# A two-layer hybrid decoder step on one core: dummy matmuls and squares at the beginning, and four edits of the recurrent mixer's order

## The chip, the cores and the metric

The kernel runs on one core of a Trainium2 chip. The time is the device time of one execution in microseconds (us); several runs are shown with their median, lowest and highest. The profile is of one execution.

## The reference

One inference step of a trunk of two layers, for a prompt of 256 tokens and 8 samples of 8 tokens (320 token columns in all), model width 1024. Every layer is a half-weighted SwiGLU network (width 2816), a mixer, and a second SwiGLU network, each with a norm before and after it:

```python
h = swiglu(rmsnorm(x, ffn1_norm_pre[l]), ffn1_w_up[l], ffn1_w_down[l])
x = x + 0.5 * rmsnorm(h, ffn1_norm_post[l])
h, cb, rh, S = mixer(rmsnorm(x, mix_norm_pre[l]), conv_st[l], rg_st[l], dn_st[l], ...)
x = x + rmsnorm(h, mix_norm_post[l])
h = swiglu(rmsnorm(x, ffn2_norm_pre[l]), ffn2_w_up[l], ffn2_w_down[l])
x = x + 0.5 * rmsnorm(h, ffn2_norm_post[l])
```

The mixer projects its input once (`h @ w_in`), runs a causal convolution of width 4 over the first columns (recurrence input, q, k, v), and joins two groups of heads:

- a gated linear recurrence of width 512 (a scan over time), times a gelu gate;
- four heads of a gated delta rule of width 128: queries, keys and values with silu, q and k of unit length; in chunks of 64 tokens a triangular system is solved, then states are carried on, `S = S * exp(gl) + (k * decay)^T @ v_new`; the output `o` is normed, `rmsnorm(o, dn_norm_w) * silu(z)`.

Both groups are concatenated and go through `w_out`. Outputs are the tokens after a final norm and all states of both layers, for the prompt and for the samples.

## The kernel before

**Numbers in two parts.** Activations lie with features on the 128 partitions, `x[128, 8, 320]`. A weight block of 1024 x 128 is loaded into a buffer `raw` by SyncE's (SP's) queue and split: ScalarE (ACT) writes the high part `wh` (L130), VectorE (DVE) the low part `wl = raw - wh` (L135). The activations are split in the same way, `xh` and `xl`. TensorE (PE) adds three products for each of 8 slices: `xh wh`, `xh wl`, `xl wh`. So one block is a *unit* of 24 matmuls of 128 x 128 by 320 columns (L158).

**Order.** PE's order is written out by hand. `Fill` (L161) holds a phase's list of units; `F(n)` issues the next n matmuls of that list and loads two units ahead (`prefetch`), `F.to(i)` all up to unit i. For the other engines a planner orders the instructions by its own forecast of when each can start: of those that are ready it takes the one that comes first in the program, and `high_priority(offset=n)` puts an instruction n places earlier. The order is then fixed, and each engine works through its own strictly. There are five `raw` buffers, three of each of `wh` and `wl`; PSUM's eight banks are three `mm`, four `sm` and one `st`.

**Beginning** (L1302 to L1423). Tokens come in rows, are transposed on PE (`xin`, L1332) and copied to `x`. The first three units are loaded in halves, and their matmuls are issued by hand, four at a time (`mm4`); ACT's and DVE's orders are written out here too. 13 dummy matmuls (`dummies`, L1327) on a constant run ahead. After them the squares of the tokens give the row factor `rs`, which PE turns (L1421) and ACT stores as `rsb2`; up to there the units' results are unscaled. `F(46)` stands between.

**Mixer** (L616 on). The list has 33 units: unit 0 is 8 columns (weights `wsr`, split into `wsh` and `wsl` in L625 and L626), then four each of k, q, v, recurrence input, z and gate, then eight of `w_out`. Each result of k, q, v and recurrence goes through `conv` (L662): two multiplications by `rsb2` on DVE (L674, L675), one step on ACT (L684), three on DVE (L686) and the copy or silu on ACT (L707, L708). Between the fill matmuls, PE runs the delta rule: products of k with k, a solve in doubling steps (`quads`, L910) whose links on ACT and DVE carry offset `HPO = 400` (called the chain below), and products of k with q (`qk`, L932, PE line L936), which need the convolved queries of all four heads. `scale_o` (L1047) computes the factor of the normed output: squares on ACT, `fs` on DVE, the power -1/2 on GpSimd (POOL), the scaling on ACT (L1057). `rg_scan` (L1073) runs the recurrence, with four roots on ACT.

The samples' state comes last: for each of two pairs of heads (p) four matmuls of 32 rows by 512 columns into four `sm` banks (L1212), added to the state by DVE (L1216), then written out by POOL's queue. `finish_o` (L1222) transposes the scaled output on PE (L1225), multiplies by silu(z) (L1227) and splits it; `split_r` (L1232) splits the recurrence output after its gate product (L735 to L737). `FL` holds the numbers of fill matmuls between these steps: `FL[19]` and `FL[20]` before each p, `FL[21]` and `FL[22]` around `finish_o`.

```python
F(FL[19 + p])
ps2 = [smtile() for _ in range(4)]
for j in range(4):
    r = slice(32 * j, 32 * j + 32)
    pe.matmul(ps2[j], kd[r, u], ve[r], start=True, stop=True)
```

Of the kernel before, what the change touches and what calls it, by code (L numbers as in the profile page):

```python
# [28 lines left out]
CVW = PADW - 3  # L29
NU = 10  # L30
HPO = 400
HPK = 300
HPW = 0
HPB = 60
# [22 lines left out]
PS = [(0, 1, 2), (0, 2, 1), (0, 2, 1)]  # L57
PO = [0, 0, -1, 0, 1, 1, -1, 2, 2, -1, 2, 1, -1]
XC = []
FL = [14, 37, 32, 9, 15, 8, 0, 14, 0, 11, 10, 8, 6, 4, 4, 6, 21, 1, 8, 0, 16, 6, 11]  # L60
FZ = [11, 11, 11, 22, 8, 17]
FY = [10, 10, 5, 3, 11, 6]

# [18 lines left out]
def trunk(ctx, tc, x_prompt, x_sample, state_conv, state_rglru, state_delta,  # L82
# [34 lines left out]
    def sttile():  # L117
        return stp.tile([128, 512], F32, name="st")

    def wload(src, r0, nk, c0, spare=False, sub=None, tok=None):  # L120
        raw = wts.tile([128, 8, 128], F32, name="raw", bufs=5)
        nc.sync.dma_start(raw[:, :nk], src[r0:r0 + nk * 128, c0:c0 + 128].rearrange("(k p) c -> p k c", p=128))
        if spare:
            w = aux.tile([128, 16, 128], F32R, name="aux")
            wh, wl = w[:, 0:8], w[:, 8:16]
        else:
            wh = wts.tile([128, 8, 128], F32R, name="wh")
            wl = wts.tile([128, 8, 128], F32R, name="wl")
        with tc.high_priority(offset=HPW):
            act(wh[:, :nk], raw[:, :nk], *((AF.Copy,) if tok is None or tok[0] else (AF.Identity, tok[1]())))  # L130
            if tok is not None and tok[0]:
                with tc.high_priority(offset=HPX):
                    stt(wl, raw, tok[1](), wh.bitcast(F32), op0=OP.add, op1=OP.subtract)
                return wh, wl
            (sub or dve).tensor_sub(wl[:, :nk], raw[:, :nk], wh[:, :nk].bitcast(F32))  # L135
        return wh, wl

    class Blk:
# [477 lines left out]
    class Mixer:  # L616
        def __init__(self, l, side):
# [4 lines left out]
            wsh = tmp.tile([128, 8, 8], F32R, name="wsh", bufs=1)  # L622
            wsl = tmp.tile([128, 8, 8], F32R, name="wsl", bufs=1)
            nc.sync.dma_start(wsr, w_in[l][:, 3072:3080].rearrange("(k p) c -> p k c", p=128))
            act(wsh, wsr, AF.Copy)  # L625
            dve.tensor_sub(wsl, wsr, wsh.bitcast(F32))  # L626
            units = [Unit(lambda a: (wsh, wsl), Blk(smtile, 8), xsplit, done=lambda ps: self.scal_done(ps))]
            for base, fn in ((1024, self.k_done), (512, self.q_done), (1536, self.v_done), (0, self.rg_done),
                             (2560, self.z_done), (2048, self.gate_done)):
                for h in range(4):  # L630
                    units.append(Unit(lambda a, c=base + 128 * h: wload(w_in[l], 0, 8, c, a, tok=(False, xtoken) if c == 512 else None), Blk(smtile if base + h == 1027 else mmtile), xsplit,
                                      done=lambda ps, h=h, fn=fn: fn(h, ps)))
            for m in range(KD):
                units.append(Unit(lambda a, m=m: wload(w_out[l], 0, 8, m * 128), Blk(mmtile if m < 3 else ptile),
# [109 lines left out]
        def run(self):  # L744
# [302 lines left out]
            def scale_o(u0, n):  # L1047
                for i in range(n):
                    act(sqtile()[:, 0:128], por[:, u0 + i], AF.Square, accum_out=oss[:, u0 + i:u0 + i + 1])
                us = slice(u0, u0 + n)  # L1050
                stt(fs[:, us], oss[:, us], 1.0 / 128, qss[:, us], op0=OP.mult, op1=OP.add)
                pool.tensor_tensor(fs[:, us], fs[:, us], mhalf[:, us], op=OP.pow)
                for i in range(n):
                    if SO:
                        dve.tensor_scalar(por[:, u0 + i], por[:, u0 + i], fs[:, u0 + i:u0 + i + 1], None, op0=OP.mult)
                    else:
                        act(por[:, u0 + i], por[:, u0 + i], AF.Copy, scale=fs[:, u0 + i:u0 + i + 1])  # L1057
# [15 lines left out]
            def rg_scan():  # L1073
# [10 lines left out]
                    stt(rt[:, c], a2, 1.0, rt[:, c], op0=OP.add, op1=OP.mult)  # L1084
                for c in range(4):
                    act(rt[:, c], rt[:, c], AF.Sqrt, scale=0.25)
                    dve.tensor_mul(it[:, c], it[:, c], rt[:, c])
                    h0 = vec[:, 2, 32 * l + c:32 * l + 32:4]
                    ts_ = mt([128, NB], "ts_", 2)
                    dve.tensor_mul(ts_, aa[:, c, NP:T:SL], h0)  # L1090
                    dve.tensor_add(it[:, c, NP:T:SL], it[:, c, NP:T:SL], ts_)
                    pool.memset(aa[:, c, 0:1], 0.0)
                    pool.memset(aa[:, c, NP:T:SL], 0.0)
                    dve.tensor_tensor_scan(xr[:, c], aa[:, c], it[:, c], 0.0, op0=OP.mult, op1=OP.add)  # L1094
# [109 lines left out]
            for p in range(2):  # L1204
                u = 8 + p
                S = SS[p]
                ve = ves[p]
                F(FL[19 + p])
                ps2 = [smtile() for _ in range(4)]
                for j in range(4):  # L1210
                    r = slice(32 * j, 32 * j + 32)
                    pe.matmul(ps2[j], kd[r, u], ve[r], start=True, stop=True)  # L1212
                for j in range(4):
                    sv4 = S[:, j // 2, 4 * (j % 2):4 * (j % 2) + 4].rearrange("p b e -> p (b e)")
                    with tc.high_priority(offset=HPO):
                        dve.tensor_add(sv4, sv4, ps2[j])  # L1216
                for h in range(2):
                    nc.gpsimd.dma_start(dn_s[l][:, 2 * p + h].rearrange("b d e -> d b e"), S[:, h])
            mh[1] = mt([128, 4, T], "kd", 1, F32R)
            ml[1] = mt([128, 4, T], "vn", 1, F32R)  # L1220
# [83 lines left out]
    raws = [wts.tile([128, 8, 128], F32, name="raw", bufs=5) for _ in range(n)]  # L1304

    def xload(c):
        nc.sync.dma_start(xtok[:, 0, c], x_prompt[0, 0:128, c])
        nc.sync.dma_start(xtok[:, 1, c], x_prompt[0, 128:256, c])
        nc.scalar.dma_start(xtok[0:64, 2, c], x_sample.rearrange("b s d -> (b s) d")[:, c])

    def whalf(i, hf):
        c0 = (i % 2) * DFF + (i // 2) * 128
# [11 lines left out]
    dve.tensor_copy(ph.gh[:, 0], bc(ones[:, 0:1], T))  # L1324
    gp0 = ph.fp.tile([128, 16], F32, name="gp0", bufs=1)

    def dummies(m):  # L1327
        ps = sttile()
        for _ in range(m):
            pe.matmul(ps[:, :T], ph.gh[:, 0, :128], ph.gh[:, 0], start=True, stop=True)  # L1330

    def xin(k):  # L1332
        ps = smtile()
# [9 lines left out]
    with tc.manual_schedule(engines={mybir.EngineType.Activation, mybir.EngineType.DVE}):  # L1343
# [27 lines left out]
        act(gp0, ps[:, 0:16], AF.Copy)  # L1371
        dummies(4)
        pt = [xin(j) for j in range(4)]
        for hf in range(2):
            k0 = 4 * hf
            xcopy(k0, pt[0])
            xcopy(k0 + 1, pt[1])
            xcopy(k0 + 2, pt[2])
            xh_(k0)
            wh_(0, hf)  # L1380
            xh_(k0 + 1)
            xcopy(k0 + 3, pt[3])
            xh_(k0 + 2)
            xh_(k0 + 3)
            wl_(0, hf)
            for i in range(1, n):
                wh_(i, hf)
            mm4(0)
            xl_(k0)
            xl_(k0 + 1)  # L1390
            mm4(0)
            if hf == 0:
                pt = [xin(4), xin(5)]
            mm4(1)
            xl_(k0 + 2)
            xl_(k0 + 3)
            mm4(2)
            wl_(1, hf)
            mm4(0)
            if hf == 0:  # L1400
                pt += [xin(6), xin(7)]
            mm4(1)
            wl_(2, hf)
            mm4(1)
            mm4(2)
            mm4(2)
        F.prefetch(5)
        ss = tmp.tile([128, 3], F32, name="rs")
        dve.memset(ss, 1.0)
        hpf = hp.rearrange("p k t -> p (k t)")  # L1410
        for t, r in enumerate((128, 128, 64)):
            act(hpf[0:r, :D], xtok[0:r, t], AF.Square, accum_out=ss[0:r, t:t + 1])
    F.i = n
    late_done, F.u[n].done = F.u[n].done, None
# [71 lines left out]
```

## Time and profile before

| | us |
|---|---|
| median of 3 runs (lowest to highest) | 1279.9 (1279.4 to 1281.31) |
| profiled execution, its own time | 1281.22 |
| its span, first to last instruction | 1279.3 |
| PE busy in the span, matmuls | 1250.1 (98%), 9812 instructions |
| DVE busy | 853.2 (67%) |
| ACT busy | 698.1 (55%) |
| POOL busy | 109.3 (9%) |
| `wl`, L135, DVE | 321 times, mean 1198 ns |
| `wh`, L130, ACT | 316 times, mean 1036 ns |
| mean granted clock of PE | 0.987 |

The page has the busy time of each engine, the span in 40 slices, DMA queues, the chain of work that ended last, and the costliest groups of instructions. Further views answer for a stretch or an engine: the timeline (start, duration, line, tile written and read, shape, count; in brackets the idle time before it and what ended it), the waits (total, times, longest), and the busy times of all engines in chosen stretches with the granted clock. Matmuls are pipelined, so their durations overlap: the distance from start to start is their cost. The low level of PE's clock is 1.2 GHz, the full one 2.4.

### The profile page before, as it was taken

Reading aid. Unit: us, or ns where it says so; the run is one execution under the profiler, and the core shown is the slowest. Engines: PE = TensorE matmul, PEld = TensorE weight load, DVE = VectorE, ACT = ScalarE, POOL = GpSimd, SP = SyncE. Lnnn points to the kernel's source line nnn. Section 1 sums busy time; section 2 is a strip of 40 time slices with the busy share of each in tenths; the row PEclk is TensorE's granted clock in tenths of the full one; section 3 lists DMA queues with packets and bytes.
Section 4 is the critical chain, followed back from the end, with each engine's and each line's share of the span. In section 5 each row is a group of like instructions: output and inputs, shape, how many; then the busy total and the mean of one; then the engine's idle time right before and its main releaser. Section 6 shows DMA issues by size and latency. Waiting matters only on the chain.

```text
span 1279.3 us, 24478 instructions
## 1 busy us (share of the span) xinstructions
PE 1250.1 (98%) x9812; PEld 1216.5 (95%) x9812; DVE 853.2 (67%) x1541; ACT 698.1 (55%) x1220; POOL 109.3 (9%) x241
## 2 busy tenths in 40 slices
PE   9999999998999999999999999999899999999996
PEld 7999999998979999999999999999899899999995
DVE  4976644799776866654486665459986877666444
ACT  5654444675686644444464444446749675444443
POOL 1100000232130100000000000013411210000000
PEclk9999999998989999999999999999999899999998
DMA  8555555563346455555645555575332655555551
GB/s 207 156 171 161 161 152 167 137 159 84 84 131 174 118 165 160 161 152 168 181 118 159 162 165 153 164 193 141 89 84 59 186 152 166 164 165 156 147 143 42
DMA packets 356470, 187.26 MB, mean 146 GB/s; under 512 B 9034, under 2 KB 353436, under 8 KB 356356
## 3 DMA queue, kind: packets, MB, share of 16 engines
q1 hardware_dynamic: 353124, 178.12, 49.3%
q0 software_dynamic: 2672, 6.65, 1.9%
q8 instruction: 77, 1.26, 0.4%
q10 hardware_dynamic: 560, 0.93, 0.2%
q14 instruction: 37, 0.30, 0.1%
HBM read 179.16 MB, written 6.51 MB: 145 GB/s over the span
## 4 chain that ended last, share of the span: by engine, by line
PE 90%; DVE 6%; ACT 2%; DMA 1%; issue 1%; POOL 0%; SPq 0%; DVEq 0%; ACTq 0%
PE mm L158 44%; PE sm L158 38%; PE sm L914 2%; PE st L231 1%; DMA raw<-in_ffn_w_up_dram 1%; PE sm L978 1%; DVE co L686 1%; DVE wl L135 1%; DVE xr L1094 1%; DVE aux L1216 0%; PE sm L936 0%; DVE nA L921 0%; DVE DN L828 0%; PE sm L1070 0%; DVE bt L425 0%
## 5 line engine op out<-in xcount | busy, mean ns | idle before, releaser
L135 DVE TENSOR_TENSOR wl<-raw,wh 128x1024 fp32r<-128x1024 f32 x321 | 384.4, 1198 | 214.1 <-ACT wh L130 209.8
L130 ACT ACTIVATE wh<-raw 128x1024 fp32r<-128x1024 f32 (+1 forms) x316 | 326.6, 1036 | 367.5 <-issue 127.0
L158 PE MATMUL mm<-xh,wl 128*128 128x320 f32 x976 | 294.8, 306 | 7.8 <-DVE wl L135 7.8
L158 PE MATMUL mm<-xh,wh 128*128 128x320 f32 x976 | 295.6, 308 | 1.0 <-ACT wh L1352 0.8
L158 PE MATMUL mm<-xl,wh 128*128 128x320 f32 x976 | 287.8, 305 | 0.0
L158 PE MATMUL sm<-xh,wh 128*128 128x320 f32 x720 | 215.6, 299 | 0.0
L158 PE MATMUL sm<-xl,wh 128*128 128x320 f32 x720 | 215.5, 299 | 0.0
L158 PE MATMUL sm<-xh,wl 128*128 128x320 f32 x720 | 215.4, 299 | 0.0
L158 PEld LDWEIGHTS mm<-xh,wl 128*128 128x128 f32 x976 | 186.2, 192 | 12.9 <-DVE wl L135 8.7
L158 PEld LDWEIGHTS mm<-xh,wh 128*128 128x128 f32 x976 | 186.7, 192 | 6.0 <-issue 1.5
L158 PEld LDWEIGHTS mm<-xl,wh 128*128 128x128 f32 x976 | 183.8, 192 | 2.7 <-issue 1.1
L158 PEld LDWEIGHTS sm<-xh,wl 128*128 128x128 f32 x720 | 136.1, 189 | 0.3 <-DVE wl L135 0.3
L158 PEld LDWEIGHTS sm<-xh,wh 128*128 128x128 f32 x720 | 136.1, 189 | 0.0
L158 PEld LDWEIGHTS sm<-xl,wh 128*128 128x128 f32 x720 | 136.1, 189 | 0.0
L158 PE MATMUL sm<-gh,wh 128*128 128x320 f32 x374 | 112.2, 300 | 0.0
L158 PE MATMUL sm<-gh,wl 128*128 128x320 f32 x374 | 111.8, 299 | 0.0
L158 PE MATMUL sm<-gl,wh 128*128 128x320 f32 x374 | 111.8, 299 | 0.0
L158 PE MATMUL mm<-gh,wh 128*128 128x320 f32 x330 | 99.0, 300 | 0.0
L158 PE MATMUL mm<-gh,wl 128*128 128x320 f32 x330 | 98.7, 299 | 0.0
L158 PE MATMUL mm<-gl,wh 128*128 128x320 f32 x330 | 98.7, 299 | 0.0
L158 PEld LDWEIGHTS sm<-gh,wl 128*128 128x128 f32 x374 | 70.7, 189 | 0.0
L158 PEld LDWEIGHTS sm<-gh,wh 128*128 128x128 f32 x374 | 70.7, 189 | 0.0
(438 smaller groups left out, 1966.3 us busy)
## 6 DMA issues: line engine op xcount, KB each, us to landing
raw<-in_ffn_w_up_dram SPq DMA_DIRECT2D x173, 512.0 KB, 3.8
raw<-in_ffn_w_down_dram SPq DMA_DIRECT2D x64, 512.0 KB, 3.9
raw<-in_w_in_dram SPq DMA_DIRECT2D x48, 512.0 KB, 4.0
raw<-in_ffn_w_down_dram SPq DMA_DIRECT2D x32, 384.0 KB, 3.4
raw<-in_w_out_dram SPq DMA_DIRECT2D x16, 512.0 KB, 3.9
aux<-in_state_delta_dram SPq DMA_DIRECT2D x8, 512.0 KB, 7.5
out_dram<-aux POOLq DMA_DIRECT2D x8, 512.0 KB, 5.3
raw<-in_ffn_w_up_dram SPq DMA_DIRECT2D x6, 256.0 KB, 7.5
```

Source lines behind the costliest of these rows:

```text
L130: act(wh[:, :nk], raw[:, :nk], *((AF.Copy,) if tok is None or tok[0] else (AF.Identity, tok[1]())))
L135: (sub or dve).tensor_sub(wl[:, :nk], raw[:, :nk], wh[:, :nk].bitcast(F32))
L158: pe.matmul(self.blk.ps(), w, il(xx), start=self.first and self.pos == 1, stop=self.last and self.pos == 3 * self.nk)
L231: pe.matmul(ps[:, t:t + 1], s[:, a:b], ones[:, 0:1], start=start and t == 0, stop=stop, skip_group_check=True)
L686: stt(co, cb[:, w:w + CVW], cwc(w), co, op0=OP.mult, op1=OP.add)
L914: pe.matmul(ps[HF[h], 64 * i:64 * i + 64], lhs(u, h), rhs(u, h), start=True, stop=True)
L978: pe.matmul(ps[32 * j:32 * j + 32, 128 * i:128 * i + 128], kz[:, h, i, c:c + 32], SS[p][:, j // 2, 4 * (j % 2) + b], start=b == 0, stop=b ...
L1094: dve.tensor_tensor_scan(xr[:, c], aa[:, c], it[:, c], 0.0, op0=OP.mult, op1=OP.add)
```

## The change

At the beginning the samples' tokens are loaded by SP's queue, ahead of the prompt's, instead of ACT's. Twenty dummies are added, six after the first transposes and fourteen among the first matmuls, and the transposes of the second half come in another place, four in a row. The squares are issued one after unit 3's load and two after unit 4's, instead of three after both. In the mixer, `wsh` takes a zero made from `rsb2` as its bias, so that it can't run before it. The low parts of `w_in`'s units get an offset of 100. The state update is done in four pairs of matmuls with two banks each and fill matmuls ahead of each. The power in `scale_o` becomes a root on ACT and a reciprocal on DVE, except in its first call; a zero from the first root of `rg_scan` is the bias of that root.

```diff
+HPL = 100
-FL = [14, 37, 32, 9, 15, 8, 0, 14, 0, 11, 10, 8, 6, 4, 4, 6, 21, 1, 8, 0, 16, 6, 11]
+FL = [14, 37, 32, 9, 15, 8, 0, 14, 0, 11, 10, 8, 6, 4, 4, 6, 21, 1, 8, 0, 8, 16, 11]
...
-            (sub or dve).tensor_sub(wl[:, :nk], raw[:, :nk], wh[:, :nk].bitcast(F32))
+            with tc.high_priority(offset=hp):
+                (sub or dve).tensor_sub(wl[:, :nk], raw[:, :nk], wh[:, :nk].bitcast(F32))
...
-            act(wsh, wsr, AF.Copy)
+            late = tmp.tile([128, 1], F32, name="tk", bufs=6)
+            dve.tensor_scalar(late, rsb2[:, 0:1], 0.0, 0.0, op0=OP.max, op1=OP.min)
+            act(wsh, wsr, AF.Identity, bias=late)
...
-                pool.tensor_tensor(fs[:, us], fs[:, us], mhalf[:, us], op=OP.pow)
+                if u0:
+                    act(fs[:, us], fs[:, us], AF.Sqrt, bias=self.tok_s)
+                    dve.reciprocal(fs[:, us], fs[:, us])
+                else:
+                    pool.tensor_tensor(fs[:, us], fs[:, us], mhalf[:, us], op=OP.pow)
...
                     act(rt[:, c], rt[:, c], AF.Sqrt, scale=0.25)
+                    if c == 0:
+                        self.tok_s = self.mt([128, 1], "toks")
+                        dve.tensor_scalar(self.tok_s, rt[:, 0, 0:1], 0.0, 0.0, op0=OP.max, op1=OP.min)
...
-                F(FL[19 + p])
-                ps2 = [smtile() for _ in range(4)]
-                for j in range(4):
-                    r = slice(32 * j, 32 * j + 32)
-                    pe.matmul(ps2[j], kd[r, u], ve[r], start=True, stop=True)
-                for j in range(4):
-                    sv4 = S[:, j // 2, 4 * (j % 2):4 * (j % 2) + 4].rearrange("p b e -> p (b e)")
-                    with tc.high_priority(offset=HPO):
-                        dve.tensor_add(sv4, sv4, ps2[j])
                 for h in range(2):
+                    F(FL[19 + p] if h == 0 else 6)
+                    ps2 = [smtile() for _ in range(2)]
+                    for j in range(2):
+                        r = slice(64 * h + 32 * j, 64 * h + 32 * j + 32)
+                        pe.matmul(ps2[j], kd[r, u], ve[r], start=True, stop=True)
+                    for j in range(2):
+                        sv4 = S[:, h, 4 * j:4 * j + 4].rearrange("p b e -> p (b e)")
+                        with tc.high_priority(offset=HPO):
+                            dve.tensor_add(sv4, sv4, ps2[j])
                     nc.gpsimd.dma_start(dn_s[l][:, 2 * p + h].rearrange("b d e -> d b e"), S[:, h])
...
     def xload(c):
+        nc.sync.dma_start(xtok[0:64, 2, c], x_sample.rearrange("b s d -> (b s) d")[:, c])
         nc.sync.dma_start(xtok[:, 0, c], x_prompt[0, 0:128, c])
         nc.sync.dma_start(xtok[:, 1, c], x_prompt[0, 128:256, c])
-        nc.scalar.dma_start(xtok[0:64, 2, c], x_sample.rearrange("b s d -> (b s) d")[:, c])
...
         pt = [xin(j) for j in range(4)]
+        dummies(6)
...
-            mm4(0)
+            for j in range(4):
+                F.u[0].mm()
+                if hf == 0:
+                    dummies((2, 3, 2, 0)[j])
             xl_(k0)
             xl_(k0 + 1)
             mm4(0)
             if hf == 0:
-                pt = [xin(4), xin(5)]
+                dummies(5)
+                pt = [xin(4)]
+                dummies(2)
+                pt += [xin(5), xin(6), xin(7)]
...
-            if hf == 0:
-                pt += [xin(6), xin(7)]
...
-        F.prefetch(5)
...
         for t, r in enumerate((128, 128, 64)):
+            F.prefetch(4 + min(t, 1))
             act(hpf[0:r, :D], xtok[0:r, t], AF.Square, accum_out=ss[0:r, t:t + 1])
```

## Rows read from the trace of the kernel before

**Rows 1.** Busy us (instructions) of each engine, clock, DMA share, GB/s; mixer stretches.

```profile
290.00:300.00 10.00, 7.86 (x67) 7.56 (x68) 8.94 (x21) 4.89 (x14) 4.60 (x10) 0.66 0.40 107
370.00:380.00 10.00, 8.32 (x29) 6.00 (x29) 9.35 (x18) 6.71 (x13) 6.69 (x8) 0.66 0.82 218
...
910.00:920.00 10.00, 6.40 (x70) 5.66 (x70) 9.97 (x25) 6.42 (x15) 4.09 (x8) 0.83 0.24 60
...
990.00:1000.00 10.00, 9.26 (x33) 5.54 (x32) 10.00 (x23) 6.39 (x14) 6.01 (x9) 0.73 0.51 131
```

**Rows 2.** PE's waits: us in total, times, longest.

```profile
PE mm L158 <- DVE wl L135: 7.8, 4, 3.5
```

**Rows 3.** Timeline of PE at the beginning.

```profile
10.27 0.64 PE L158 MATMUL mm<-xh,wh 128*128 128x320 f32 x1 [0.75 <-ACT wh L1352]
...
12.45 1.27 PE L158 MATMUL mm<-xh,wl 128*128 128x320 f32 x4
...
20.22 0.71 PE L158 MATMUL mm<-xl,wh 128*128 128x320 f32 x4
...
26.74 0.43 PE L158 MATMUL sm<-xh,aux 128*128 128x320 f32 x2
...
34.72 0.60 PE L1421 MATMUL sm<-ident,rs 128*128 128x128 f32 x3 [1.57 <-DVE rs L237]
```

**Rows 4.** Timeline of ACT at the beginning.

```profile
26.08 0.26 ACT L625 ACTIVATE wsh<-wsr 128x64 fp32r<-128x64 f32 x1 [2.02 <-DMA wsr<-in_w_in_dram]
...
32.90 1.05 ACT L1412 ACTIVATE hp<-xtok 64x1024 f32<-64x1024 f32 x1
```

**Rows 5.** Timeline of PE, first mixer, early place.

```profile
292.14 0.64 PE L158 MATMUL mm<-xh,wl 128*128 128x320 f32 x1 [3.46 <-DVE wl L135]
...
294.17 1.91 PE L936 MATMUL sm<-qa,ka 128*128 128x128 f32 x8
...
298.31 0.40 PE L158 MATMUL mm<-xl,wh 128*128 128x320 f32 x1
```

**Rows 6.** Timeline of DVE there.

```profile
275.74 1.22 DVE L135 TENSOR_TENSOR wl<-raw,wh 128x1024 fp32r<-128x1024 f32 x1
...
287.50 3.46 DVE L686 SCALAR_TENSOR_TENSOR co<-cb,vec,co 128x344 f32<-128x344 f32 x7
290.87 1.22 DVE L135 TENSOR_TENSOR wl<-raw,wh 128x1024 fp32r<-128x1024 f32 x1
```

**Rows 7.** Timeline of SP there: the next weight transfer's issue.

```profile
277.02 0.37 SPq L122 DMA_DIRECT2D raw<-in_w_in_dram  x1
```

**Rows 8.** Timeline of ACT there: the last of the queries.

```profile
293.03 0.33 ACT L708 ACTIVATE qa<-co,tok 128x64 f32<-128x64 f32 x1
```

**Rows 9.** All engines in the same stretch, columns as in rows 1.

```profile
286.61:294.17 7.56, 3.96 (x50) 3.52 (x45) 7.56 (x17) 6.36 (x14) 3.39 (x8) 0.82 0.08 19
```

**Rows 10.** Timeline of PE, first mixer, late place.

```profile
365.38 1.14 PE L1212 MATMUL sm<-nA,kd 32*128 32x512 f32 x8
366.45 0.40 PE L158 MATMUL mm<-xh,wh 128*128 128x320 f32 x1
...
369.24 1.86 PE L1212 MATMUL sm<-at,kd 32*128 32x512 f32 x4 [0.35 <-DVE hp L1091]
...
376.08 1.11 PE L1225 MATMUL sm<-ident,qa 128*128 128x128 f32 x4 [1.48 <-DVE aux L1216]
...
389.24 0.30 PE L158 MATMUL mm<-kd,wh 128*128 128x320 f32 x1
```

**Rows 11.** All engines in the late place, columns as in rows 1.

```profile
365.13:389.86 24.73, 22.70 (x130) 18.76 (x129) 23.47 (x48) 18.96 (x40) 7.49 (x10) 0.86 0.61 172
```

**Rows 12.** Timeline of DVE: the last gated channel.

```profile
392.69 0.49 DVE L1234 TENSOR_TENSOR qa<-xr,vo 128x320 fp32r<-128x320 f32 x1 [0.54 <-ACT vo L1233]
```

**Rows 13.** Timeline of ACT: the Silus' table and the Silus.

```profile
375.11 1.28 ACT L1198 ACT_TABLE_LOAD   x1
376.41 1.92 ACT L1198 ACTIVATE ka<-ka,tok 128x320 f32<-128x320 f32 x4
```

More of the change, by code (lines that the diff above doesn't have):

```diff
@@ L118, in sttile, with wload @@
         return stp.tile([128, 512], F32, name="st")
-    def wload(src, r0, nk, c0, spare=False, sub=None, tok=None):
+    def wload(src, r0, nk, c0, spare=False, sub=None, tok=None, hp=0):
         raw = wts.tile([128, 8, 128], F32, name="raw", bufs=5)
@@ L630, in __init__ @@
                 for h in range(4):
-                    units.append(Unit(lambda a, c=base + 128 * h: wload(w_in[l], 0, 8, c, a, tok=(False, xtoken) if c == 512 else None), Blk(smtile if base + h == 1027 else mmtile), xsplit,
+                    units.append(Unit(lambda a, c=base + 128 * h: wload(w_in[l], 0, 8, c, a, tok=(False, xtoken) if c == 512 else None, hp=HPL), Blk(smtile if base + h == 1027 else mmtile), xsplit,
                                       done=lambda ps, h=h, fn=fn: fn(h, ps)))
@@ L1325, in trunk @@
     gp0 = ph.fp.tile([128, 16], F32, name="gp0", bufs=1)
+    dps = []
     def dummies(m):
-        ps = sttile()
+        dps[:] = dps or [sttile()]
         for _ in range(m):
-            pe.matmul(ps[:, :T], ph.gh[:, 0, :128], ph.gh[:, 0], start=True, stop=True)
+            pe.matmul(dps[0][:, :T], ph.gh[:, 0, :128], ph.gh[:, 0], start=True, stop=True)
     def xin(k):
```

## The prediction

> **What bounds the kernel now.** I read the page first. TensorE (PE) is the bound: one weight matmul follows another for nearly the whole span, so a change is worth what it takes out of PE's idle time, and out of the time in which PE runs at the lower of its two clock levels. I then asked for the busy time of each engine in 10 us stretches. The feed-forward stretches are full, at full clock. The losses sit in the two mixers, at one early and one late place each: PE 7.86 to 9.26 us busy of 10 (6.40 at the worst), granted clock 0.66 to 0.83, and VectorE (DVE) at 8.94 to 10.00 [rows 1]. A granted clock of 0.66 over 10 us is 6.8 us at half clock (1.2 instead of 2.4 GHz), so some 3.4 us of work lost on top of the idle time. Third, PE's waits: the low parts of weights (`wl`, L135) cost 7.8 us in four waits, the longest 3.5 [rows 2]. The timeline of each place says what is late there.
>
> Beginning [rows 3]: PE waits 0.75 us for the first weights. Four matmuls take 1.27 us at 12.45 and 0.71 at 20.22, the last one's tail included; from start to start that is 0.267 against 0.136 us each, the pace of 1.2 and of 2.4 GHz. PE had run dummies, transposes and matmuls with small gaps before the clock rose, at about 18 us. Three units are done at 26.74, and at 34.72 PE has waited 1.57 us for `rs`, because the squares on ScalarE (ACT) run as late as 32.90; ACT had stood 2.02 us waiting for the transfer of `wsr` at 26.08 [rows 4].
>
> Early place, first mixer [rows 5 to 7]: PE waits 3.46 us for a `wl`, restarts at 292.14 at 0.267 us a matmul, and is through the next chain step at 298.31. That `wl` ran at 290.87, behind seven convolution steps (3.46 us from 287.50). Weights come late for the same reason: the `wl` of 275.74 ends at 276.97, and the next weight transfer is issued at 277.02, when this `wl` has freed its raw buffer.
>
> Late place [rows 10 to 12]: the first state update (four matmuls) takes 365.38 to 366.45. The second, from 369.24, comes in pieces as banks come free (1.86 for its first two); then 1.48 us are lost at the output transposes, at 376.08, and the clock is down [rows 1]. The output projection starts at 389.24. DVE is busy 23.47 of the 24.73 us to 389.86, where its last gate product begins.
>
> **The change part by part.** The sum is made against the profiled execution's 1281.2 us (span 1279.3, 1.9 around it), 1.3 above the runs' median of 1279.9; gains are then taken off the median.
>
> *Early squares and `wsh`.* `wsh` moves behind the row factor, so its wait for a transfer leaves ACT's queue; the squares move one weight earlier. They then end some 5 us sooner (2.0 of wait, three weight parts of about 1 us that now follow), `rs` is ready long before PE asks, and the 1.57 goes: **gain 1.6**. What is late next are the weights of the following units; DVE's work there starts with `rsb2` and shifts with it. The new token is one DVE step of some 0.15; `wsr`'s second transfer waits longer on SP's queue, with raw weights behind it, but those wait for buffers until later anyway. Without that cover it costs the wait and an issue's 0.37.
>
> *Dummies, and the samples' transfer on SP's queue.* Two more issues on SP at 0.37 [rows 7] put prompt tokens and weights up to 0.8 later; ACT's queue loses them. Twenty dummies are added: 5.3 us at 0.267, 2.7 at 0.136. Six fill the 0.75 wait; the rest stand in line with real matmuls. Against that, work goes at half the time from the moment the clock rises. From 9.5 us I count 92 matmuls (72 real, 20 dummies) and four groups of transposes (0.97 us cold, about 0.6 warm). Clock up at 18 as before: done at about 28.5, a loss of 1.8. Up near 12.9: 26.1, a gain of 0.6; up at once: limited by ACT and DVE to about 25, a gain of 1.7. **I take 0**, between; both ends stay for the range.
>
> *Low parts first.* Each `wl` of the input projection overtakes the convolution steps of the last units, though not the chain (its offset is 100 against 400). The transfer behind it goes out earlier, and the 3.46 wait goes. Late next are the queries' convolutions: the product of k and q, the next thing on PE, needs the last query at 293.36 [rows 8] and started at 294.17. DVE has no idle time between the chain's end at 286.61 and 294.17 [rows 9], and it owes nine convolution steps (0.49 each) before that query. If the `wl` still runs in this stretch, ahead of them, the last query stays at 293.4: gain 0.8. If it has gone before 286.6, in one of DVE's holes, the query comes 1.2 sooner: gain 2.0. If two go ahead of the nine steps: loss 0.4. With nothing late behind it: 6.2, since 288.5 to 298.3 holds 3.6 us of work at full clock. **I take 1.4 for each layer, 2.8.**
>
> *Four pairs.* No row shows a pair. Four matmuls take 1.07, the piece of two that waited for a bank 1.86 [rows 10], so a pair costs between half of the one and half of the other, 0.53 to 0.93; I take 0.93, the nearer in form: 4 x 0.93 - 2 x 1.07 = 1.6 us more PE work a layer. The Trainium skill ("TensorE: Matmul & The Clock Gate", Part 3: Packing small matmuls) says that tiles on different row groups run side by side, so two would take about as long as four; by that a layer pays 2.1 and not 1.6. The four in 1.07 agree with it; no run here shows two. In return, only two banks are held at a time, with 6 to 8 fill matmuls between, so the waits and the low clock go. PE's own work from 365.38 to the output projection is then 96 x 0.136 + 4 x 0.93 + 1.1 of transposes + 0.4 of gaps = 18.3 against 23.9: 5.6 less.
>
> But DVE does not become faster. It has 1.26 us idle in this stretch [rows 11] and gets some 0.55 more (two reciprocals, a token), so the last gate product, at 389.86 before, comes at best at 389.15, and the last gated channel (392.69 [rows 12]) about 1.5 sooner where the `wl` between them goes behind it, 0.5 where it doesn't. PE used that channel at 389.24 + 35 x 0.136 = 394.0, 0.8 after it was done. **Gain 1.3 to 2.4; I take 1.8 a layer, 3.6**; the ends are -1.6 (pairs paid, nothing gained) and 5.6.
>
> *Root and reciprocal.* Two powers on GpSimd become a root on ACT and a reciprocal on DVE, small tiles all. The last scaling ends sooner, but the Silus behind it then wait for the token that DVE gives after the scan's last root, so I cost it at nothing beyond the 0.55. It adds waits: behind the reciprocal on DVE stand the state's additions, for which PE's banks wait, and behind the root on ACT stand the Silus.
>
> Sum: 1.6 + 0 + 2.8 + 3.6 = 8.0. 1281.2 - 8.0 = 1273.2 in the profile's terms, **1272** as a median.
>
> **The rivals.**
> *All waits go and the clock stays up.* For it: PE idles only at the places that the edits touch. Against it: DVE at 8.9 to 10.0 there. 1.6 + 6.2 + 5.3 (second mixer: 3.6 idle and 1.7 by its 0.83) + 5.6 + 4.9 (0.7 less, by 0.73 against 0.66) = 23.6: 1256.
> *The waits only move.* The queries and the last gate become the new waits, as long and as cold, and the dummies eat the squares' gain: 1278 to 1280. For it: DVE's full stretches, and the 0.8 us that separate both next waits from the old ones.
> *Slower: the root falls behind the Silus' table.* If a root of the last scaling comes after the load of the Silu table (1.28 at 375.11, then 1.92 of Silus [rows 13]), the table is loaded twice more and the reciprocal holds DVE for 2 x 1.28 + 1.92 = 4.5 us, with additions and low parts behind it. DVE has no room there, so PE pays: 9.0 - 1.6 = 7.4 more, 1287. Against it: the Silus wait for a token from after the scan's last root. It decides as soon as one root of the scaling stands behind that load. The Trainium skill ("ScalarE: Activation LUTs", What ACT_TABLE_LOAD costs) gives 2.66 us for a switch; with that this rival is at 1293. The trace has 1.28, and the next activation starts 1.30 after the load does, so the trace's price stands.
>
> **How the numbers follow.** Forecast 0.52 (its own range 1267 to 1277), all waits gone 0.23, waits moved 0.14, slower 0.11. Leaving out the lower half of the second and most of the last gives 1257 to 1281. What this measurement tells from no change is about 0.2%, 2.6 us. Faster: the forecast but for 0.03, the second, and 0.03 of the third: 0.75. Same: 0.03 and most of the third: 0.14. Slower: 0.11.
>
> **What would show it.** Right: no wait at L1421; squares before 28 us; no PE wait on `wl` in the mixers, and weight transfers there issued earlier; a wait of 2 to 4 us for the queries (L936) in its place, still with a low clock behind it; the four pairs without waits for banks; PE waiting for a low part or a gated channel early in the output projection. Wrong: full clock through both mixers (second case); three units done after 29 us (dummies too dear); another table load between the scan's roots and the Silus, and DVE waiting 4 us at the reciprocal (fourth).

## The result

| | before | changed |
|---|---|---|
| median, us (runs) | 1280.6 (4) | 1297.4 (1296.6 to 1299.0, 4) |
| ratio, 95% interval | | 1.0135 [1.0122, 1.0147] |
| profiled span, us | 1279.3 | 1294.8 |
| PE busy, us | 1250.1 | 1256.9 |

The change costs 16.8 us. The forecast was a gain of 8.0, so even the sign is wrong, and none of the rivals was the one that came.

**Where it goes.** PE's order is written by hand, so the same matmul can be found in both traces. The difference of its two start times, taken at a few points of the kernel before, says what each stretch lost (us, minus is a gain):

| kernel | beginning (to 70) | early, mixer 1 | late, mixer 1 | early, mixer 2 | late, mixer 2 |
|---|---|---|---|---|---|
| changed | +1.0 | +4.5 | +1.8 | +4.0 | +4.1 |
| `hpl_only` | -0.8 | +3.9 | +0.3 | +5.1 | +1.0 |
| `pairs_only` | +2.8 | -1.3 | -1.4 | -0.1 | -0.6 |
| `root_only` | -1.0 | -0.5 | -0.2 | -0.2 | 0.0 |
| `squares_only` | -2.1 | -1.3 | -0.1 | 0.0 | 0.0 |
| `beginning_only` | +5.2 | 0.0 | 0.0 | 0.0 | 0.0 |
| `no_lowparts` | +0.6 | 0.0 | -1.1 | 0.0 | -0.1 |
| `no_root` | +1.4 | +2.6 | +1.8 | +3.7 | +2.6 |
| `pairs_squares_offset10` | -2.1 | -2.6 | -1.4 | +0.7 | -0.6 |

The points are the early place's end at 305 us, 360, 405, 880, 925, 986 and 1030. The changed kernel's row sums to 15.4, against 15.5 in the spans. Each row is one execution: a stretch that no edit touches moves by up to 1.3 where the low clock behind a wait lasts longer or shorter (early, mixer 1, in `pairs_only` and `squares_only`), and the beginning by more (last section). The profiled execution of `pairs_only` was the slowest of its ten, those of `beginning_only` and `no_root` the slowest too. Not in the table is the stretch from 405 to 880, in which `pairs_only` and `no_lowparts` lose 1.1 near 638 us (last section). So signs of parts below that size rest on the medians further down.

**The profile after.** First the stretches that answer to [rows 1], the columns as there.

```profile
270.00:280.00 10.00, 8.86 (x57) 8.67 (x58) 7.41 (x23) 5.01 (x8) 1.77 (x6) 0.83 0.46 123
290.00:300.00 10.00, 5.21 (x60) 4.02 (x59) 10.00 (x23) 6.22 (x15) 4.14 (x8) 0.90 0.49 121
300.00:310.00 10.00, 10.00 (x133) 9.23 (x134) 7.50 (x17) 4.04 (x10) 2.10 (x8) 0.76 0.13 38
380.00:390.00 10.00, 8.33 (x62) 7.87 (x60) 6.54 (x17) 8.24 (x16) 2.13 (x4) 1.00 0.78 253
920.00:930.00 10.00, 5.22 (x52) 3.95 (x48) 10.00 (x22) 5.87 (x15) 4.33 (x9) 0.80 0.57 154
```

PE is busy 5.21 and 5.22 us in stretches where DVE has no idle time at all. In the early place of mixer 1 (the first three rows) the clock costs 1.7, 1.0 and 2.4 us of work, 5.1 in all, against 3.4 in [rows 1]. The last two are one fall, which the row of 296 to 306 has whole:

```profile
296.00:306.00 10.00, 6.79 (x61) 6.26 (x62) 8.80 (x23) 3.56 (x10) 3.53 (x10) 0.66 0.41 107
```

Next, PE's waits, to be read against [rows 2]:

```profile
PE sm L940 <- ACT qa L711: 9.2, 6, 2.5
PE mm L160 <- DVE wl L137: 4.1, 4, 1.4
PE mm L160 <- DVE cb L679: 2.3, 3, 1.0
```

The low parts' 7.8 us are down to 4.1, and none of that is in the early places. (Another 1.4 is at the beginning, where `sm` banks are written.) The queries, which cost nothing before, cost 9.2: three waits in each layer. PE in the early place of mixer 1 [rows 5]:

```profile
273.13 0.37 PE L160 MATMUL mm<-xh,wh 128*128 128x320 f32 x1 [1.01 <-DVE cb L679]
...
292.66 0.40 PE L160 MATMUL mm<-xh,wl 128*128 128x320 f32 x1
...
294.57 0.49 PE L940 MATMUL sm<-qa,ka 128*128 128x128 f32 x2 [0.47 <-ACT qa L711]
...
296.68 0.49 PE L940 MATMUL sm<-qa,ka 128*128 128x128 f32 x2 [1.62 <-ACT qa L711]
...
299.70 0.80 PE L940 MATMUL sm<-qa,ka 128*128 128x128 f32 x2 [2.53 <-ACT qa L711]
```

and DVE there [rows 6]:

```profile
273.24 1.23 DVE L137 TENSOR_TENSOR wl<-raw,wh 128x1024 fp32r<-128x1024 f32 x1 [0.26 <-ACT wh L131]
...
291.42 1.18 DVE L137 TENSOR_TENSOR wl<-raw,wh 128x1024 fp32r<-128x1024 f32 x1
292.52 2.03 DVE L690 SCALAR_TENSOR_TENSOR co<-cb,vec,co 128x344 f32<-128x344 f32 x4
294.47 1.22 DVE L137 TENSOR_TENSOR wl<-raw,wh 128x1024 fp32r<-128x1024 f32 x1
295.61 1.06 DVE L690 SCALAR_TENSOR_TENSOR co<-cb,vec,co 128x344 f32<-128x344 f32 x2
296.58 1.22 DVE L137 TENSOR_TENSOR wl<-raw,wh 128x1024 fp32r<-128x1024 f32 x1
297.71 0.57 DVE L690 SCALAR_TENSOR_TENSOR co<-cb,vec,co 128x344 f32<-128x344 f32 x1
```

The low part that PE once waited 3.46 us for is in time (292.66 has no wait). But three low parts now stand between the steps of the last queries, 3.6 us in all. Earlier, others stand among the decay steps that begin the chain and among the copies that free banks (1.01 at 273.13), so the chain itself starts 3 to 3.5 us later (the beginning's 1.0 taken off); that shift alone takes back what the wait gave.

The late place, PE, DVE and ACT [rows 10, 13]:

```profile
370.82 1.13 PE L1224 MATMUL sm<-nA,kd 32*128 32x512 f32 x4
371.88 0.40 PE L160 MATMUL mm<-xh,wh 128*128 128x320 f32 x1
...
390.04 0.58 PE L160 MATMUL mm<-xh,wl 128*128 128x320 f32 x1 [1.36 <-DVE wl L137]
...
395.77 0.37 PE L160 MATMUL mm<-kd,wh 128*128 128x320 f32 x1 [0.39 <-DVE bt L739]
```

```profile
375.27 1.22 DVE L137 TENSOR_TENSOR wl<-raw,wh 128x1024 fp32r<-128x1024 f32 x1
...
378.39 1.22 DVE L137 TENSOR_TENSOR wl<-raw,wh 128x1024 fp32r<-128x1024 f32 x1
...
380.12 0.81 DVE L1105 TENSOR_TENSOR_SCAN xr<-vo,hp 128x320 f32<-128x320 f32 x1
...
381.44 0.22 DVE L1055 SCALAR_TENSOR_TENSOR fs<-oss,qss 128x4 f32<-128x4 f32 x2
...
387.30 0.15 DVE L733 TENSOR_SCALAR tok<-ka 128x1 f32<-128x1 f32 x1 [3.36 <-ACT ka L1209]
```

```profile
381.62 0.48 ACT L1057 ACTIVATE fs<-fs,toks 128x4 f32<-128x4 f32 x2 [6.65 <-DVE fs L1055]
...
385.35 1.92 ACT L1209 ACTIVATE ka<-ka,tok 128x320 f32<-128x320 f32 x4
```

Two low parts pass the third and the fourth scan, the factor's sum falls behind the last scan, ACT stands 6.65 us, and then DVE, the engine that limits this place, stands 3.36 us for the Silus. In the kernel before, DVE waited 0.54 us there:

```profile
378.36 0.15 DVE L729 TENSOR_SCALAR tok<-ka 128x1 f32<-128x1 f32 x1 [0.54 <-ACT ka L1198]
```

The beginning, PE and ACT [rows 3, 4]:

```profile
7.40 0.47 PE L1348 MATMUL sm<-ident,xtok 128*128 128x128 f32 x1 [1.17 <-DMA xtok<-in_x_prompt_dram]
...
27.77 0.43 PE L160 MATMUL sm<-xh,aux 128*128 128x320 f32 x2
...
34.02 0.58 PE L1439 MATMUL sm<-ident,rs 128*128 128x128 f32 x3
...
55.81 0.40 PE L160 MATMUL sm<-xh,wl 128*128 128x320 f32 x1 [1.02 <-DVE wl L137]
```

```profile
28.16 1.04 ACT L1430 ACTIVATE hp<-xtok 64x1024 f32<-64x1024 f32 x1
...
40.26 0.35 ACT L629 ACTIVATE wsh<-wsr,tk 128x64 fp32r<-128x64 f32 x1 [3.04 <-DMA wsr<-in_w_in_dram]
```

The wait for `rs` is gone, as forecast. PE waits for the prompt's tokens instead, and `wsh` still waits for its transfer, only later and ahead of the first gated values.

### The profile page after: what moved, and what is told of

Read it like the earlier page. It is cut to its first block, busy times and chain, and to the rows that moved or that the text cites. A ratio compares the mean times of both kernels' runs of the same rounds, so it can differ in the third digit from the quotient of the medians.

```text
span 1294.8 us, 24526 instructions
## 1 busy us (share of the span) xinstructions
PE 1256.9 (97%) x9832; PEld 1219.6 (94%) x9832; DVE 854.1 (66%) x1549; ACT 697.0 (54%) x1224; POOL 98.5 (8%) x237
## 3 DMA queue, kind: packets, MB, share of 16 engines
q0 software_dynamic: 2672, 6.65, 1.9%
## 4 chain that ended last, share of the span: by engine, by line
PE 83%; DVE 10%; ACT 3%; DMA 2%; issue 2%; SPq 1%; POOL 0%; DVEq 0%; ACTq 0%
PE mm L160 39%; PE sm L160 36%; DVE wl L137 2%; PE sm L918 2%; DVE co L690 1%; DMA raw<-in_ffn_w_up_dram 1%; PE st L233 1%; PE sm L982 1%; ACT qa L1065 0%; DVE xr L1105 0%; DVE aux L1228 0%; DMA wsr<-in_w_in_dram 0%; DVE nA L925 0%; PE sm L1078 0%; DVE bt L427 0%
```

## The experiments

All times are medians beside runs of the kernel before on the same chip (1279.8 to 1280.4 there); a difference is against those.

**Each part alone.** `hpl_only`, the offset of the low parts:

```diff
+HPL = 100
+            with tc.high_priority(offset=hp):
+                (sub or dve).tensor_sub(wl[:, :nk], raw[:, :nk], wh[:, :nk].bitcast(F32))
```

> The kernel before with one edit: the low parts of the input projection's weights get the offset 100. Theory: the early places lose what the changed kernel loses there, 4.4 us in the first mixer and 4.0 in the second, because three low parts (1.22 us each) run ahead of the last queries' convolutions; the late places lose 0 to 2 us each. 1280.6 + 8.4 to 12.4 = 1289 to 1293, with PE waits of 6 to 9 us in all for the queries. Rival: the queries are late only because the beginning shifts the planner's order; then this edit alone gives the gain of 2.8 that was forecast, 1278, and no wait for the queries above 2 us.

1292.1, ratio 1.0093 [1.0077, 1.0109]: +11.9. PE waits 8.7 us for the queries:

```profile
PE sm L938 <- ACT qa L709: 8.7, 6, 2.2
```

The theory holds in place, and the size is at the upper end. As in the changed kernel, three low parts stand among the last nine convolution steps on DVE. This one edit loses more than two thirds of what the whole loses.

`pairs_only` (the loop over h with two banks, `FL[20]` and `FL[21]`):

> The kernel before with one edit: the state update in four pairs with the new fill counts. Theory: a pair takes PE as long as four matmuls (1.06 us in the changed kernel), so 2.1 us of PE work a layer are added; of the waits for banks and the half clock some 1.5 to 3 a layer go: 1279 to 1282, about no change. Rival one, the forecast: 1.8 a layer are gained, 1277. Rival two, the pairs carry the late places' loss of 5.9 us of the changed kernel: 1286.5.

1277.8, ratio 0.9985 [0.9975, 0.9995]: 2.4 faster, between the theory and the forecast. A pair occupies PE for 1.06 us until the next fill matmul starts:

```profile
366.93 1.13 PE L1213 MATMUL sm<-nA,kd 32*128 32x512 f32 x4
367.99 0.40 PE L158 MATMUL mm<-xh,wh 128*128 128x320 f32 x1
```

So 2.1 us of PE work a layer are paid (4 x 1.06 less 2 x 1.07), and the late places still gain 1.4 and 0.6.

`root_only` (root on ACT, reciprocal on DVE, token from the scan's first root):

> The kernel before with one edit: output factor of the last heads by root and reciprocal, with the token from the scan's first root. Theory: in the planned order the sum for the factor on DVE now falls behind the scans and the state's additions, so ACT stands idle for 4 to 7 us before the root, the Silus start 2 to 3.5 us later and DVE waits for them: 2 to 3 us a layer lost, 1284 to 1287. Rival, the forecast: nothing, 1280 to 1281, the factor's sum on DVE before the third scan as now. Rival two: root and Silu tables alternate, 33 or more table loads instead of 31, and 1287.

1280.5, ratio 1.0006 [0.9996, 1.0015]: no change, the forecast was right and my theory wrong. Alone, the factor's sum stays ahead of the fourth scan and ACT waits 2.47 us, as it waited for the power before:

```profile
370.54 0.48 ACT L1053 ACTIVATE fs<-fs,toks 128x4 f32<-128x4 f32 x2 [2.47 <-DVE fs L1051]
```

`squares_only` (prefetch between the squares, token for `wsh`):

> The kernel before with one edit: squares one weight earlier, the small weight's high part behind the row factor by a token. Theory: the 1.57 us wait for the row factor goes, but the high part's wait for its transfer (3.0 us in the changed kernel, at 40 us) now stands on ACT ahead of the first gated values, and PE waits 1.4 us for low parts at 56 and 60 us: net 0 to -0.3, 1280.3 to 1280.6. Rival, the forecast: 1.6 gained, 1279.0, no wait for a low part before 65 us.

1278.8, ratio 0.9986 [0.9977, 0.9996]: 1.3 faster, the forecast's 1.6 less 0.3. Here `wsh` does not wait at all: its transfer is issued at 21.40, in the changed kernel not before 34.63.

```profile
21.40 0.39 SPq L624 DMA_DIRECT2D wsr<-in_w_in_dram  x1
```

**Parts undone, and the queries first.** `no_lowparts` is the changed kernel with no offset on `wl`, `no_root` with the powers back on POOL. `lowparts_queries_first` is `hpl_only` with `high_priority(offset=200)` around the queries' copies, convolution steps and activations. `beginning_only` has the samples' transfers on SP's queue, the dummies and the earlier transposes.

> The changed kernel without the offset of the low parts; all else of the change stands. Theory: the offset alone makes the early places late (3.9 and 5.1 us with it alone) and it is also what pushes the factor's sum behind the scans in the late places, so without it early places go back to the kernel before (-1.3 to 0 each), late places gain about 1 each as with the pairs alone (-1.4, -0.6), and the beginning keeps its +1.0: 1277 to 1281. Rival: the late places' loss (1.8 and 4.1) comes from pairs and root together; then 5.9 of it stay: 1285 to 1287, ACT idle over 4 us before the root.

1282.0, ratio 1.0017 [1.0008, 1.0027]. That is 2.2 above the kernel before where the changed kernel is 16.8 above: 14.6 us come back by one offset. The late places gain again or lose nothing (-1.1 and -0.1) with pairs and root both in. That refutes the rival.

> The changed kernel with the two powers on GpSimd instead of root and reciprocal; all else stands. Theory: low parts and root together make the late loss (the factor's sum on DVE moves behind the last scan only where both are in); without the root the four-column sum is back before the third scan, and the late places come to about the sum of the two edits alone, -1.1 and +0.4, so 6.6 us less than the changed kernel: 1290 to 1292, early places unchanged at +4 to +5 each. Rival: the two low parts ahead of the third and fourth scan are enough to hold Silu and gates; then 1295 to 1298.

1292.5, ratio 1.0097 [1.0082, 1.0113]. The median is 0.5 above what was expected, but that is luck, since the stretches are not as expected: the late places keep +1.8 and +2.6, where I had the two edits' sum, -1.1 and +0.4. So the low parts ahead of the scans and the pairs are enough for most of the late loss. DVE waits 1.93 us for the Silus here, against 3.36 with the root:

```profile
384.20 0.15 DVE L733 TENSOR_SCALAR tok<-ka 128x1 f32<-128x1 f32 x1 [1.93 <-ACT ka L1202]
```

> The kernel before with the low parts at offset 100, and the queries' convolutions (copies, steps, last activations) at 200, ahead of the low parts. Theory: the early loss of the low parts alone is the three that run ahead of the last queries; with the queries first the waits for them (8.7 us in six) fall under 2 us, and the wait for the low part (3.5 us a layer) stays gone: early places -2 to +1 each instead of +3.9 and +5.1, late +0.3 and +1.0: 1278 to 1284. Rival: DVE is simply full there, so that whatever goes first, something else is as late (a low part, the chain): early places +3 to +5 each, 1288 to 1293.

1288.6, ratio 1.0073 [1.0057, 1.0088]: the rival's time, and in part its mechanism. Queries and low parts are in time, and the keys, the head of the chain, are late (PE's waits in the early place of mixer 1):

```profile
PE sm L863 <- ACT ka L713: 4.7, 1, 4.7
```

The early places cost less in this trace (+0.4 and +1.8) than the median says, and less than the rival's +3 to +5; part of the rest is a beginning that lost 2.1 without an edit in it.

> The kernel before with the beginning's edits alone: samples' transfer on SP's queue, 20 dummies, transposes brought forward. Theory: the prompt's tokens land 1.2 us later behind the samples, the dummies stand in line with real work, and the full clock comes 3 us sooner without paying for it: +0.5 to +1.5, 1281.1 to 1282.1. Rival, the forecast: 0, 1280.6. Rival two: the sooner clock wins, -0.5 to -1.7, 1279 to 1280.

1284.4, ratio 1.0040 [1.0028, 1.0053]: worse than each theory. PE waits for the prompt, and on ACT `wsh` waits 5.92 us with the copy of the row factor (`rsb`) queued behind it:

```profile
9.24 0.48 PE L1337 MATMUL sm<-ident,xtok 128*128 128x128 f32 x1 [3.19 <-DMA xtok<-in_x_prompt_dram]
```

```profile
40.43 0.26 ACT L625 ACTIVATE wsh<-wsr 128x64 fp32r<-128x64 f32 x1 [5.92 <-DMA wsr<-in_w_in_dram]
40.60 0.42 ACT L1429 ACTIVATE rsb<-sm 128x320 f32<-128x320 f32 x1
```

**The parts that gain, a small offset, and the beginning split.** `pairs_and_squares` has these two edits alone; `pairs_squares_offset10` adds `HPL = 10`; `samples_order_only` and `dummies_only` split the beginning.

> The kernel before with the four pairs and the early squares, nothing else of the change. Theory: the two edits lie 300 us apart and add: -2.4 and -1.3 as measured alone, 1276.4 (1275.4 to 1277.4), faster than the kernel before and the fastest so far; no offset of low parts, so no wait for the queries. Rival: the pairs' gain was a luckier phase of the half clock (one stretch of it fewer), not less waiting; then about 1278.5 with the late places at 0.

1278.3, ratio 0.9985 [0.9977, 0.9994]. 1.7 faster, less than the sum of the two; this is the rival's time without its mechanism, since its trace has the late places at -1.4 and -0.6, as with the pairs alone, and not at 0. Why the two do not add is not settled.

> As the last one, with an offset of 10 for the low parts instead of 100: in the order on DVE one low part now stands three convolution steps earlier and none passes a scan. Theory: VectorE is full in the early place, so a low part that goes first is paid for by the queries: early places -0.5 to +1.5 each, late as without it; 1276 to 1279. Rival: the offset was only too large, and a small one gives the forecast's 1.4 a layer: 1273 to 1274.

1274.9, ratio 0.9955 [0.9942, 0.9968]: 5.1 faster than before, the best of all. In the early place the wait for the low part is 2.01 where it was 3.46, and the queries' product starts without a wait:

```profile
288.59 0.52 PE L160 MATMUL mm<-xh,wl 128*128 128x320 f32 x1 [2.01 <-DVE wl L137]
...
290.50 1.85 PE L940 MATMUL sm<-qa,ka 128*128 128x128 f32 x8
```

The difference to `pairs_and_squares` is 3.4 in the medians, about what the forecast had for the low parts (2.8); my theory here, no gain to speak of, was wrong. The waits agree with it: for low parts PE waits 2.4 us in the early place of each mixer, against 3.9 before. The two places' times in the trace (-2.6 and +0.7) differ by more than that because the low clock behind the wait is shorter in mixer 1 than before (granted 0.91 against 0.83 over 284 to 304) and longer in mixer 2 (0.83 against 0.91 over 905 to 925).

> The kernel before with one edit: the samples' transfers of both halves issued on SP's queue, ahead of the prompt's. Theory: this is the beginning's loss (4.6 us with the whole beginning): PE waits 1 to 4 us for the prompt's tokens, 1282 to 1284. Rival: two issues of 0.4 us each, 1280 to 1281, and the dummies carry the loss.

1281.9, ratio 1.0013 [1.0004, 1.0022], between theory and rival, with 1.9 us of waiting for the prompt. And SP's planned order changes with it: `wsr` goes out at 34.74, behind the raw weights, instead of 21.87.

```profile
34.74 1.67 SPq L624 DMA_DIRECT2D wsr<-in_w_in_dram  x1
```

> The kernel before with the 20 dummies and the transposes brought forward, the samples' transfers left on ACT's queue. Theory: PE does not wait for tokens, the full clock comes sooner, and what dummies cost and the clock gives about cancel: -0.5 to +1, 1279.5 to 1281. Rival: the dummies carry the beginning's loss, 1283 to 1285.

1279.9, ratio 0.9995 [0.9986, 1.0004]: no change, `wsr` issued at 21.84. So the beginning loses nothing without the order of transfers. That order does two things: PE waits for the prompt, and `wsr` is issued 13 us later. The late `wsr` is in the traces of all six kernels with that order (34.3 to 35.4), and in none of the eleven others (21.0 to 22.2). With the dummies too, the two cost 4.6, more than 1.9 and -0.2 together. The traces show a reason: in `samples_order_only` `wsh` stands on ACT behind the copy of the row factor, and waits 2.40 there; in `beginning_only` it stands ahead of that copy, which comes at 40.60.

```profile
35.44 0.44 ACT L1422 ACTIVATE rsb<-sm 128x320 f32<-128x320 f32 x1 [1.42 <-PE sm L1421]
```

What the prompt's wait and the late `wsr` cost each was not separated.

**How large the offset may be.** The changed kernel with `HPL = 10`, the same with the samples back on ACT's queue, and pairs and squares with `HPL = 20`:

> The changed kernel with the low parts' offset at 10 instead of 100, one number. Theory: the offset is the whole loss of the mixers; early places come to -2.6 and +0.7, late to -1.1 and -0.1 as without the offset, the beginning keeps +0.6 to +1.0: 1282.0 without low parts, less 3.4, so 1278.6 (1277 to 1280). Rival: with root and pairs in, low parts hurt at any offset: 1282 or more.

1280.6, ratio 0.9995 [0.9982, 1.0009]: with one number changed, the 16.8 us are gone. It is 2 slower than expected. Its profiled execution (1278.6) has the mixers about as expected (-2.6, -0.9, -1.2, -0.1) and the beginning at +1.8.

> As the last one, and the samples' transfers back on ACT's queue. Theory: the order of transfers is what the beginning loses (PE waited 1.2 to 3.9 us for the prompt in each kernel that has it); 2 to 4.6 us less than the last one: 1274 to 1277. Rival: the dummies are what the beginning loses once the squares are early; then no more than 0.5 less than the last one.

1278.8, ratio 0.9986 [0.9976, 0.9995]: another 1.8, just under the 2 expected at least; its ten runs spread over 2.4 us, those of the last one over 6.9. What parts it from the 1274.9 are root and dummies, which alone cost +0.3 and -0.2; why the two cost 3.9 here is open. With the root in, PE waits 1.8 us in the two late places for the pairs' banks, against 0.9.

> Pairs, early squares and offset 20: in the order on DVE two low parts, not one, stand ahead of the last queries' steps, and one more ahead of a low part's place in the late place. Theory: each low part ahead of the queries costs them 1.2 us and PE has 0.8 to spare, so early places lose 1 to 2.5 us each against offset 10: 1277 to 1280. Rival: the loss at 100 comes from the low parts that stand among the earlier steps (softplus, bank copies), not from the queries; then 20 is within 1 us of 10.

1281.7, ratio 1.0007 [0.9996, 1.0018]: 6.4 more than offset 10, above what I expected. PE's waits in the early place of mixer 1, first at 20, then at 10:

```profile
PE sm L940 <- ACT qa L711: 2.1, 1, 2.1
PE mm L160 <- DVE wl L137: 2.0, 1, 2.0
```

```profile
PE mm L160 <- DVE wl L137: 2.4, 2, 2.0
```

The second low part ahead of the queries costs 2.1 and gives nothing: the wait for the first low part is as long as at 10. This profiled execution (1278.3) was the fastest of its ten runs, so these rows explain the sign and not all of the 6.4.

## Why the prediction was wrong

**The step that failed is "low parts first"**: +1.4 a layer, with a loss of 0.4 as the worst bound. Alone it loses 11.9 in the median; by the trace 3.9 and 5.1 in the early places. Its premises were measured well: no idle time on DVE, the queries next, 0.8 us of slack. Two conclusions from them were not. First, I counted which low parts could overtake the nine convolution steps of [rows 9], took one as likely and two as the worst case, and did not work out that an offset of 100 places takes three. The forecast said where the new wait would stand and nearly its size (2 to 4 us; it is 4.6 in each layer), but booked it as a remainder of the old one and not as a cost. Second, the bound looked only at 286 to 294. The offset holds for every weight of the input projection: the ones at 264 to 274 delay the head of the chain by 3 to 3.5 us, and those at 375 and 378 pass the scans. With offset 10, beside pairs and squares, where one low part moves three steps and none passes a scan, the step gives 3.4, about the forecast's 2.8; alone it was not run.

**Four pairs.** The price was taken as 0.93 us for a pair, half of the 1.86 in [rows 10]; but that row is already one pair with a wait in it, so its half bounds nothing. A pair takes 1.06, and the Trainium skill's rule ("TensorE: Matmul & The Clock Gate", Part 3: Packing small matmuls), which I cited and set aside, has it right: two row groups take about as long as four, 2.1 us a layer. A wait for banks was to go and stays: in the changed kernel the last pair keeps PE from 377.47 to 379.50, with a wait of 0.7 for a bank. Alone the edit gains 2.4 and not 3.6. With low parts first nothing of it is left: the late places have -1.1 and +0.4 as the sum of the two edits' traces, and +1.8 and +2.6 in `no_root`, which has both.

**Root and reciprocal.** Costed at nothing, and alone it is nothing (+0.3 in the median, the interval holds 1). The slower rival, roots behind the Silu table, did not come: the profile has 31 table loads before and after. What came with the other edits is a third thing: in the planned order the factor's sum went behind the last scan. The low parts alone do half of that: in `hpl_only` and `no_root` the sum's last two columns go behind the last scan, the first four stay ahead of the third. That the Silus wait for the root then is shown (6.65, 3.36); that the root adds 1.5 in mixer 2 and 0.0 in mixer 1 is the difference of two traces and not more. By the medians the root out gives 4.1; where the rest of it comes from is open.

**Early squares.** Right by mechanism, 1.3 alone for 1.6. In the changed kernel one premise failed: with `wsh` behind the row factor, "its wait for a transfer leaves ACT's queue". There the first transfer of `wsr` is itself 13 us later, by another edit, and `wsh` waits 3.04 for it after all. The term had looked only at the second transfer.

**The beginning** is the second term that failed: 0, between a loss of 1.8 and a gain of 1.7, and 4.6 lost alone. The dummies, on which its working was spent, are the part that was right (-0.2): in `dummies_only` matmuls go at 0.136 from 14.3 us on and the three units are done at 26.95, where the kernel before has about 18 and 26.74. That lies between the prediction's cases of 12.9 and 18, and cost and gain cancel. The transfer order had one sentence, "up to 0.8 later"; it is 1.2 to 3.9 us of waiting in the six traces, and the shift of `wsr`, an instruction that the edit does not touch, was not in the sum.

So of the terms 1.6, 0, 2.8 and 3.6 the first is right alone (1.3), the last two thirds right (2.4), and the second and third are losses of 4.6 and 11.9. Interactions cost the rest: the parts measured alone add up to +13.1 (11.9 - 2.4 + 0.3 - 1.3 + 4.6), the whole is +16.8. In the changed kernel the low parts stand for 14.6 of it.

## What to carry to other kernels

A priority that overtakes has to be counted in the order itself: write down which instructions stand behind it on a full engine, for every place where the same helper runs, before a gain is booked; then try the smallest offset that moves the one late instruction. Where an engine has no idle time, a wait that goes is a wait that comes elsewhere, unless work is removed, moved into a hole, or what is overtaken has slack (0.8 us here). And an edit of a planned order can move instructions that it does not name, so each part is worth a run by itself.

## What the runs showed of the hardware

Two matmuls of 32 rows on two row groups keep PE for 1.06 us, four on four row groups for 1.07.

The beginning varies from run to run by more than the mixers. With the same instructions up to 25 us, PE waited 0.8 us for the first weights before, and 2.6 with the pairs alone. In the five traces whose beginning has no edit, the three units are done between 25.0 (`root_only`) and 27.7 us (`pairs_only`).

```profile
PE mm L158 <- ACT wh L1352: 2.6, 1, 2.6
```

The low clock behind one and the same wait lasts differently. With the squares alone, PE waits 3.47 us for the low part, as before, and restarts at 289.99; the granted clock of the ten us from there is 0.83, against 0.66 in [rows 1]:

```profile
290.00:300.00 10.00, 10.00 (x123) 9.52 (x124) 10.00 (x23) 4.29 (x12) 4.14 (x10) 0.83 0.47 126
```

That is 1.7 us of work that one execution loses and another does not. Four traces, all with the pairs, also run at the lower level for a moment near 638 us, where PE had only a short gap; five others with the pairs do not. `pairs_and_squares` comes first, `pairs_squares_offset10` below it.

```profile
630.00:640.00 10.00, 9.44 (x62) 9.30 (x61) 7.03 (x12) 4.58 (x9) 0.00 (x0) 0.85 0.95 262
```

```profile
630.00:640.00 10.00, 9.33 (x69) 8.82 (x68) 7.11 (x16) 4.86 (x11) 0.00 (x0) 1.00 0.73 200
```

PE is as busy in both, and what decides between them was not tried. Single profiles of this kernel cannot tell apart edits smaller than 1 to 2 us; medians of ten runs can, to about 1 us.
